# Summing the last three units of each expert stage with one-hot matmuls behind the loop, and one pair of modulation weights moved to the end of layer 0

## The chip, the cores and the metric

One core of one Trainium2 chip runs the whole kernel in one launch. The metric is the device time in microseconds. A core has TensorE (PE, with its weight loads shown apart as PEld), VectorE (DVE), ScalarE (ACT), GpSimd (POOL) and SyncE (SP, which here issues nearly all transfers). Each engine works through its own queue in order; semaphores tie the queues together.

## What is computed

Two layers over 256 latent and 256 context tokens of width 1024. Each layer has a mixer (an S5 state-space group, latent attention, an mLSTM group, then an output projection and a norm) and a mixture of 64 experts, top 8, with one shared expert. Both are modulated by rows that a small matmul makes from `c`. Cut to what matters here:

```python
for layer in range(DEPTH):
    mod_lat = silu(c) @ ada_w[layer] + ada_b[layer]
    mod_ctx = silu(c_ctx) @ ada_w[layer] + ada_b[layer]
    sh1, sc1, g1, sh2, sc2, g2 = split(mod_lat[:, None, :], 6)
    h_lat = _layer_norm(x_lat) * (1 + sc1) + sh1
    z_lat = h_lat @ w_in[layer]                    # projections, then S5, attention, mLSTM
    ...
    y_lat = concatenate([s5_lat, mla_lat, ml_lat]) @ w_out[layer]
    x_lat = _layer_norm(ALPHA * x_lat + g1 * y_lat, ln1_g[layer], ln1_b[layer])
    f_lat = _layer_norm(x_lat) * (1 + sc2) + sh2
    ffn_lat = _moe(f_lat, ...)                     # sum over a token's experts of gate * expert(f)
    x_lat = _layer_norm(ALPHA * x_lat + g2 * ffn_lat, ln2_g[layer], ln2_b[layer])
```

The context stream goes through the same steps in layer 0 and is not needed behind the mixer of layer 1. So the expert stage of layer 0 has 512 tokens (four tiles of 128), that of layer 1 has 256 (two tiles).

## The kernel before

**Units and scatters.** The router ranks the experts by load; `plan(l)` puts one to four ranks together into a *unit* of one or two tiles of at most 128 rows. Per unit POOL gathers the rows (L1779), PE makes gate and up (L1822) from expert weights that SP streams into the slots of `ring`, then down (L1835), and ACT and DVE write the gated rows to a tile `xo` (L1839, L1840). POOL then adds the rows of `xo` to the tokens' rows of `Y` in HBM by an indirect scatter with add (L1845), one for each expert's rows; each waits until the one before has landed. `units` is walked in the order of the plan. Over its last six turns `merging` puts alpha times the old rows and the shared expert's part times `g2` into `acc`.

**The last unit of layer 1.** Its rows are not scattered. `fold` makes one-hot tiles (128 rows by tokens), sums the rows per token on PE (L1914), multiplies by `g2` (L1915) and adds to `acc` (L1916). In layer 0 there is no such step.

**The loop.** `spilled` (L1924, L1925) is a loop over experts whose rows did not fit into the plan; it normally makes no turn. Its entry is passed by all engines together, when what stands ahead of it on each queue, the transfers included, is done. In layer 0 the program puts the last two scatters behind it.

**The combination.** `combine`, per tile of 128 tokens: SP loads its rows of `Y` (L2011), POOL multiplies them by `g2` (L2016), DVE adds `acc` and takes the row sums (L2019). The norm: mean on DVE (L416, L417), squares on ACT (L419), root on POOL (L420, L421), scale and shift on DVE (L427, L428). In layer 0 a second norm of the result follows, whose row ACT writes (L2030); PE transposes it (L313), and ACT and DVE modulate the transposed tile `hT` (L457, L459). The tiles run interleaved, each some steps behind the one before. Then PE does the projections of layer 1 (L466).

**Modulation.** `ada_pair(l, g)` makes two of the six modulation rows: eight steps, in each a load of 1 MB of `ada_w` by SP and four matmuls (L365). The loads share four places of 1 MB with the weights of the projections and of the output projection. In layer 1 `more` runs the pairs 1 and 2 inside the attention, and then loads `w_out`.

## Time and profile before

| | |
|---|---|
| median of 3 runs | 1956.22 us (1953.4 to 1962.03) |
| the profiled execution | 1952.31 us |
| span of its trace | 1950.3 us |
| PE busy | 1792.0 us, 92% |
| DVE, ACT, POOL busy | 775.7, 394.1, 453.5 us |
| mean granted clock of PE | 0.962 |

The profile comes from one execution. Its page gives each engine's busy time, the span in forty slices, the transfers, and the costliest groups of instructions by line. The trace behind it gives the timeline of a stretch: start, duration, engine, line, operation, tile written <- tiles read, and in brackets how long the engine had stood idle before and what ended that. xN says that N instructions of one kind stand in a row together. A granted clock of 1.00 is 2.4 GHz, one of 0.50 is 1.2 GHz. Names are those of the program; `cat`, `sw` and `spare` are buffers in which, at the end of a layer, rows of `Y` stand.

### The profile page before, as it was taken

Reading aid. Unit: us, or ns where it says so; the run is one execution under the profiler, and the core shown is the slowest. Engines: PE = TensorE matmul, PEld = TensorE weight load, DVE = VectorE, ACT = ScalarE, POOL = GpSimd, SP = SyncE. Lnnn points to the kernel's source line nnn. Section 1 sums busy time; section 2 is a strip of 40 time slices with the busy share of each in tenths; the row PEclk is TensorE's granted clock in tenths of the full one; section 3 lists DMA queues with packets and bytes.
Section 4 is the critical chain, followed back from the end, with each engine's and each line's share of the span. In section 5 each row is a group of like instructions: output and inputs, shape, how many; then the busy total and the mean of one; then the engine's idle time right before and its main releaser. Section 6 shows DMA issues by size and latency. Waiting matters only on the chain. (4 is left out here: it accounts for less than half of the span.)

```text
span 1950.3 us, 29070 instructions
## 1 busy us (share of the span) xinstructions
PE 1792.0 (92%) x10161; PEld 843.7 (43%) x10161; DVE 775.7 (40%) x2252; ACT 394.1 (20%) x756; POOL 453.5 (23%) x453
## 2 busy tenths in 40 slices
PE   6999999979999999999998089899899999999993
PEld 2654665533443433334332056665544444444330
DVE  5656664852422332222221386564722222322113
ACT  2345332301111111111111143531311111011000
POOL 3120211232232232223221570002011111112223
PEclk8999999989999999999999589899899999999997
DMA  8442568299999899999997425258599999996882
GB/s 327 143 98 102 180 242 304 81 337 348 342 335 336 323 304 350 371 352 350 341 365 269 130 74 107 97 217 307 189 417 366 350 345 332 340 370 200 320 296 88
DMA packets 158305, 523.98 MB, mean 269 GB/s; under 512 B 28862, under 2 KB 42110, under 8 KB 149452
## 3 DMA queue, kind: packets, MB, share of 16 engines
q1 hardware_dynamic: 139612, 480.36, 66.6%
q0 software_dynamic: 18544, 41.73, 9.7%
q8 instruction: 82, 1.34, 0.3%
q14 instruction: 67, 0.55, 0.1%
HBM read 531.12 MB, written 47.51 MB: 297 GB/s over the span
## 5 line engine op out<-in xcount | busy, mean ns | idle before, releaser
L1822 PE MATMUL gu<-ring,xT 128*32 128x512 f32 (+3 forms) x2896 | 653.4, 599 | 8.7 <-DMA ring<-in_exp_w 8.6
L1822 PEld LDWEIGHTS gu<-ring,xT 128*32 128x32 f32 (+3 forms) x2896 | 194.2, 128 | 372.0 <-issue 313.0
L1835 PE MATMUL dn<-ring,hT 128*32 128x512 f32 (+3 forms) x1448 | 319.2, 598 | 1.3 <-DVE hT L1726 1.0
L1845 POOL DMA_INDIRECT Y<-xo,gi x79 | 119.9, 1518 | 557.9 <-DMA Y<-xo,gi 129.0
L1718 DVE TENSOR_TENSOR hh<-gu,sg 128x256 f32<-128x256 f32 (+3 forms) x86 | 36.4, 425 | 496.5 <-ACT sg L1717 496.4
L1835 PEld LDWEIGHTS dn<-ring,hT 128*32 128x32 f32 (+3 forms) x1448 | 98.7, 128 | 178.3 <-issue 159.7
L1845 POOL DMA_INDIRECT Y<-xo,si x66 | 90.1, 1365 | 318.0 <-DMA Y<-xo,gi 216.5
L1840 DVE TENSOR_SCALAR xo<-dn,gc 128x512 f32<-128x512 f32 (+3 forms) x80 | 60.1, 751 | 229.5 <-PE dn L1835 221.4
L1717 ACT ACTIVATE sg<-gu 128x256 f32<-128x256 f32 (+3 forms) x86 | 32.8, 384 | 563.4 <-PE gu L1822 545.4
L466 PE MATMUL pT<-hT,w 128*128 128x512 f32 (+1 forms) x288 | 119.1, 566 | 2.5 <-ACT hT L457 2.5
L1797 PEld LDWEIGHTS <-fb 128*128 128x128 bf16 x1536 | 86.5, 99 | 55.0 <-issue 55.0
L1839 ACT ACTIVATE xo<-dn,gc 128x512 f32<-128x512 f32 (+3 forms) x80 | 55.0, 687 | 222.1 <-PE dn L1835 217.6
L1797 PE MATMUL xT<-oneh,fb 128*128 128x128 bf16 (+4 forms) x1536 | 97.3, 220 | 0.0
L1799 ACT COPY xT<-xT 128x512 f32<-128x512 f32 (+3 forms) x80 | 45.8, 573 | 219.4 <-PE xT L1797 137.4
L1429 PE MATMUL yo<-w,cat 128*128 128x512 f32 x192 | 83.3, 593 | 0.7 <-DMA w<-in_w_out 0.7
L1799 DVE COPY xT<-xT 128x512 f32<-128x512 f32 (+3 forms) x80 | 53.4, 670 | 76.5 <-PE xT L1797 43.6
L466 PEld LDWEIGHTS pT<-hT,w 128*128 128x128 f32 x288 | 55.4, 197 | 54.8 <-issue 48.0
L313 PE MATMUL hT<-cst,xt 128*128 128x128 f32 x64 | 14.0, 386 | 61.9 <-DMA w<-in_w_uv 50.8
L1779 POOL DMA_INDIRECT xg<-fd,gi x48 | 51.3, 1068 | 67.6 <-PE xT L313 33.7
L365 PE MATMUL ada<-w,sil 128*32 128x512 f32 x384 | 56.8, 650 | 10.4 <-DMA w<-in_ada_w 10.4
L474 PE MATMUL pN<-w,hT 128*128 128x256 f32 (+2 forms) x256 | 61.0, 395 | 0.0
L313 PEld LDWEIGHTS xT<-cst,xg 128*128 128x128 f32 (+4 forms) x384 | 41.1, 140 | 38.8 <-issue 36.3
(565 smaller groups left out, 2053.1 us busy)
## 6 DMA issues: line engine op xcount, KB each, us to landing
ring<-in_exp_w SPq DMA_DIRECT2D x768, 512.0 KB
w<-in_ada_w SPq DMA_DIRECT2D x48, 1024.0 KB
w<-in_w_out SPq DMA_DIRECT2D x8, 1024.0 KB
sw<-in_sh_w SPq DMA_DIRECT2D x2, 3072.0 KB
w<-in_w_uv SPq DMA_DIRECT2D x4, 1024.0 KB
Y<-zeros SPq DMA_DIRECT2D x8, 512.0 KB
w<-in_w_mm SPq DMA_DIRECT2D x4, 1024.0 KB
w<-in_w_qk SPq DMA_DIRECT2D x4, 768.0 KB
```

The source lines that it names most:

```text
L313: self.nc.tensor.transpose(out, in_, self.c("ident")[:in_.shape[0], :in_.shape[0]])
L365: nc.tensor.matmul(ps[32 * q:32 * q + 32, :], self.sil[:, k, :], t[:, q * 512:(q + 1) * 512], start=k == 0, stop=k == 7, tile_position=(0, ...
L466: self.nc.tensor.matmul(ps[base:base + m, n0:NT], w[k][:, col:col + m], hT[:, k, n0:NT], start=k == 0, stop=k == 7)
L474: self.nc.tensor.matmul(ps[:, :n], hT[:, k, i * 128:(i + 1) * 128], w[k][:, col:col + n], start=k == 0, stop=k == 7)
L1429: nc.tensor.matmul(st[at][n], cb[:, i * 128:(i + 1) * 128], wo[n][b], start=b == 0, stop=b == 7)
L1797: nc.tensor.matmul(o, self.fb[i][:, z, cs], t["oh"][:, i, 0:m], start=at == 0, stop=at + 1 == len(parts))
L1799: (nc.scalar.copy if hh else v.tensor_copy)(o, a)
L1822: nc.tensor.matmul(t["gu"][r, :], t["xt"][:, 2 * c + b, r], ws[j][:, b * 512:(b + 1) * 512], start=c == 0 and b == 0, stop=c == 3 and b == ...
L1835: nc.tensor.matmul(po[n][r, :], t["ht"][:, b, r], ws[b * nr + j][:, n * 512:(n + 1) * 512], start=b == 0, stop=b == 1, **kw)
L1839: nc.scalar.activation(xo[0:m, 0:512], po[0][0:m], AF.Identity, scale=t["gc"][0:m])
L1840: v.tensor_scalar(out=xo[0:m, 512:1024], in0=po[1][0:m], scalar1=t["gc"][0:m], scalar2=None, op0=OP.mult)
L1845: nc.gpsimd.indirect_dma_start(out=self.Y[l], out_offset=bass.IndirectOffsetOnAxis(ap=si[0:cap], axis=0), in_=xo[col:col + cap], in_offset ...
```

## The change

Constant `FOLD = 3`: the rows of the last three units of either layer are not scattered. In layer 0 that takes away four scatters, in layer 1 five (its last unit was not scattered before either).

When the third unit from the end has had its turn, what is left of `merging` is drained, POOL itself issues the loads of `Y` (four in layer 0, two in layer 1), and `add_y` on POOL multiplies each by `g2` and adds it to `acc`. `backs` makes the one-hot tiles on DVE in the last turn. Behind the loop `fold` sums the three units' rows per token on PE, six matmuls per tile, DVE writes them times `g2` into the tile's place, and the sum with `acc` follows as before.

The ring's pool is closed right behind the loop. At the end of layer 0 the pools of layer 1 open there, and the pair (1, 1) of modulation is run interleaved with the combination; the small constants and the first projection weights are loaded behind its weights. In the attention of layer 1 only the pair (1, 2) is left. Some pools of layer 1 open later or close later.

```diff
+FOLD = 3
...
+            self.zp, self.gp = P(zs, "z"), P(zs, "gates")
...
-        for j, g in ((0, 1), (0, 2), (1, 0)) if l == 0 else ((1, 1), (1, 2)):
+        for j, g in ((0, 1), (0, 2), (1, 0)) if l == 0 else ((1, 2),):
...
-                if l and u is units[-1]:
+                if u in units[-FOLD:]:
                     t["xo"] = xo
                     continue
...
-        for _ in merge:
-            pass
+            if i == n - FOLD:
+                for _ in merge:
+                    pass
+                for k, y in enumerate(self.yb):
+                    nc.gpsimd.dma_start(y, self.Y[l][k * 128:(k + 1) * 128])
+                for add in self.adds:
+                    add()
+            if i == n - 1:
+                self.backs(l, units[-FOLD:], rp, len(self.yb))
...
+    def backs(self, l, units, rp, nt):
+        v = self.nc.vector
+        for k, t in enumerate(t for u in units for t in u["tiles"]):
...
+            for i0 in range(0, nt, 2):
+                v.tensor_scalar(out=t["back"][0:m, i0:i0 + 2], in0=self.c("iota1")[0:m, 0:256].rearrange("p (a b) -> p a b", a=2),
+                                scalar1=128.0 * i0 - 4097.0, scalar2=at[0:m], op0=OP.add, op1=OP.is_equal)
...
+    def add_y(self, y, acc, g2):
+        p = self.nc.gpsimd
+        p.tensor_tensor(out=y, in0=y, in1=g2, op=OP.mult)
+        p.tensor_tensor(out=acc, in0=acc, in1=y, op=OP.add)
+
+    def fold(self, i, units, g2):
...
+        ts = [t for u in units for t in u["tiles"]]
+        y = self.yb[i]
+        for n in range(2):
+            ps, cs = self.bank("fold"), slice(n * 512, (n + 1) * 512)
+            for x, t in enumerate(ts):
+                nc.tensor.matmul(ps, t["back"][0:t["m"], i], t["xo"][0:t["m"], cs], start=x == 0, stop=x + 1 == len(ts))
+            v.tensor_tensor(out=y[:, cs], in0=ps, in1=g2[:, cs], op=OP.mult)
...
-            if last:
-                self.fold(l, units[-1], rp, acc, sw, tiles)
             self.spilled(l, fT, acc, sw, rp, ring, tiles)
...
+            er.close()
+            ahead = iter(())
+            if not last:
+                self.begin(l + 1)
+                self.ada = self.ada_pair(l + 1, 1, self.adp)
+
+                def ahead():
+                    for k in range(8):
+                        next(self.ada)
+                        if k % 2:
+                            yield
+                    self.fetch(l + 1)
+                ahead = ahead()
+            with self.tc.tile_pool(name=f"comb{l}", bufs=1) as pp:
+                weave(*(self.combine(l, i, t, pp, self.yb[i], acc, sw, 2 * i, len(tiles), units[-FOLD:]) for i, t in enumerate(tiles)), ahead)
+                if not last:
+                    weave(self.ada)
...
-        nc.sync.dma_start(a, self.Y[l][i * 128:(i + 1) * 128])
-        for _ in range(lag):
+        for _ in range(i):
             yield
-        if l == 0 and i == 1:
-            self.fetch(l + 1)
-        nc.gpsimd.tensor_tensor(out=a, in0=a, in1=sw[:, 2 if t >= 2 else 3], op=OP.mult)
-        yield
+        self.fold(i, units, sw[:, 2 if t >= 2 else 3])
+        for _ in range(lag - i):
+            yield
```

In the order of the instructions, POOL at the end of layer 0 looked like this before: scatters from `xo` (`gi` and `si` are the lists of rows), the loop (L1924, L1925) and two more scatters; behind these, after three memsets, come the products of the combination (L2016).

```order
L1845 DMA Y_78<-xo,si 640x1024
L1845 DMA Y_78<-xo,gi 640x1024 x2
L1924 TENSOR_LOAD ovl
L1925 COMPARE_AND_BRANCH
L1925 UNCONDITIONAL_BRANCH x2
L2078 BRANCH_PREFETCH_HINT
L1925 REGISTER_ALU
L1925 COMPARE_AND_BRANCH
L1925 UNCONDITIONAL_BRANCH
L1845 DMA Y_78<-xo,gi 640x1024
L1845 DMA Y_78<-xo,si 640x1024
```

Now the last scatters are followed by four loads of `Y` (L1892) and the eight products and sums of `add_y` (L1925, L1926), and the loop (L1945) stands behind them.

```order
L1850 DMA Y_78<-xo,gi 640x1024
L1850 DMA Y_78<-xo,si 640x1024
L1892 DMA cat_1334<-Y_78 128x1024 x3
L1892 DMA sw<-Y_78 128x1024
L1925 TENSOR_TENSOR cat_1334<-cat_1334,sw 128x1024 x2
L1926 TENSOR_TENSOR acc<-acc,cat_1334 128x1024 x2
L1925 TENSOR_TENSOR cat_1334<-cat_1334,sw 128x1024
L1925 TENSOR_TENSOR sw<-sw 128x1024
L1926 TENSOR_TENSOR acc<-acc,cat_1334 128x1024
L1926 TENSOR_TENSOR acc<-acc,sw 128x1024
L1945 TENSOR_LOAD ovl
```

So POOL's products moved from behind the loop to ahead of it, its sums are new, and four scatters are gone.

PE leaving that loop, before: the transposes of the combination's rows (L313), then the projections of layer 1.

```order
L1925 REGISTER_ALU
L1925 COMPARE_AND_BRANCH
L1925 UNCONDITIONAL_BRANCH
L313 MATMUL hT<-cst,xt 128x128 x32
L466 MATMUL pT<-hT,w 128x512 x16
L474 MATMUL pN<-w,hT 128x256 x16
```

And now, where L1936 are the summing matmuls (six for a tile), L367 the modulation matmuls (four for a step), and L315 the transposes:

```order
L1936 MATMUL fold<-xo,xT 128x512 x6
L367 MATMUL ada<-w,sil 32x512 x4
L1936 MATMUL fold<-xo,xT 128x512 x3
L367 MATMUL ada<-w,sil 32x512 x4
L1936 MATMUL fold<-xo,xT 128x512 x3
L367 MATMUL ada<-w,sil 32x512 x8
L315 MATMUL hT<-cst,xt 128x128 x8
L1936 MATMUL fold<-xo,xT 128x512 x6
L367 MATMUL ada<-w,sil 32x512 x8
L1936 MATMUL fold<-xo,xT 128x512 x6
L367 MATMUL ada<-w,sil 32x512 x4
L315 MATMUL hT<-cst,xt 128x128 x4
```

Four more modulation matmuls, the other twenty transposes and the projections follow. All summing and all eight steps now stand ahead of most transposes; eight transposes of the first tile stand ahead of the third and the fourth tile's summing.

SP behind the same loop now begins with modulation weights and the stores of `x2d` (L2049); the weights of the projections (L354) come behind them.

```order
L365 DMA w<-in_ada_w 128x2048 x4
L2049 DMA x2d<-acc 128x1024
L365 DMA w<-in_ada_w 128x2048 x2
L2049 DMA x2d<-acc 128x1024
L365 DMA w<-in_ada_w 128x2048 x2
L1239 DMA cols<-in_cols 128x20
L1240 DMA mlg<-in_ml_g 128x256
L354 DMA w<-in_w_uv 128x2048 x2
L354 DMA w<-in_w_go 128x1344 x2
L2049 DMA x2d<-acc 128x1024 x2
```

Before, four loads of `Y`, the small constants and two of these weights stood there first.

## Rows read from the trace of the kernel before

**Rows 1.** The page: part 1 (busy us, share, instructions), a line of part 2 (forty slices).

```profile
PE 1792.0 (92%) x10161; PEld 843.7 (43%) x10161; DVE 775.7 (40%) x2252; ACT 394.1 (20%) x756; POOL 453.5 (23%) x453
...
GB/s 327 143 98 102 180 242 304 81 337 348 342 335 336 323 304 350 371 352 350 341 365 269 130 74 107 97 217 307 189 417 366 350 345 332 340 370 200 320 296 88
```

**Rows 2.** Stretch: length; busy us of PE, PEld, DVE, ACT, POOL; clock, DMA, GB/s.

```profile
1080.00:1120.00 40.00, 1.05 (x5) 1.05 (x6) 17.70 (x27) 7.31 (x11) 21.70 (x18) 0.50 0.49 147
```

**Rows 3.** Timeline, end of layer 0: start, us, engine, line, tiles, [idle before <-releaser].

```profile
1065.81 2.34 PE L1835 MATMUL dn<-ring,hT 128*32 128x512 f32 x20
...
1073.22 1.44 POOL L1845 DMA_INDIRECT Y<-xo,gi  x1 [2.94 <-DMA Y<-xo,si]
...
1092.51 1.37 POOL L1845 DMA_INDIRECT Y<-xo,si  x1 [4.41 <-DMA Y<-xo,gi]
...
1095.87 1.28 SPq L2011 DMA_DIRECT2D cat<-Y  x3
```

**Rows 4.** Waits of SP from 1040 to 1100: us in total, times, longest.

```profile
SPq L1925 <- DMA Y<-xo,gi: 12.3, 2, 7.1
...
SPq L2011 <- DMA Y<-xo,si: 10.4, 1, 10.4
```

**Rows 5.** Timeline of the combination behind layer 0.

```profile
1099.16 7.92 POOL L2016 TENSOR_TENSOR cat<-cat,sw 128x1024 f32<-128x1024 f32 x3 [2.63 <-DMA cat<-Y]
...
1101.54 3.34 DVE L2019 SCALAR_TENSOR_TENSOR cat<-cat,acc 128x1024 f32<-128x1024 f32 x1 [32.48 <-DMA cat<-Y]
...
1109.81 2.33 POOL L2016 TENSOR_TENSOR sw<-sw 128x1024 f32<-128x1024 f32 x1
...
1116.11 0.57 POOL L421 TENSOR_TENSOR a0rs<-a0rs,mhalf 128x1 f32<-128x1 f32 x1
...
1117.48 1.22 DVE L2019 SCALAR_TENSOR_TENSOR sw<-sw,acc 128x1024 f32<-128x1024 f32 x1
...
1117.65 1.24 ACT L2030 ACTIVATE xt<-acc,nb,a0rs 128x1024 f32<-128x1024 f32 x1 [0.62 <-DVE nb L2029]
...
1118.95 1.97 PE L313 MATMUL hT<-cst,xt 128*128 128x128 f32 x8 [50.80 <-DMA w<-in_w_uv]
...
1133.56 15.79 PE L466 MATMUL pT<-hT,w 128*128 128x512 f32 x32
```

**Rows 6.** The page, part 5 (busy us, mean ns of one): POOL's gathers.

```profile
L1779 POOL DMA_INDIRECT xg<-fd,gi x48 | 51.3, 1068 | 67.6 <-PE xT L313 33.7
```

**Rows 7.** Timeline at the end of layer 1.

```profile
1904.51 1.34 POOL L1845 DMA_INDIRECT Y<-xo,gi  x1 [6.20 <-DMA Y<-xo,si]
...
1914.19 3.70 PE L1914 MATMUL fold<-xo,xT 128*128 128x512 f32 x8 [0.84 <-ACTq L1925]
...
1915.18 1.51 POOL L1845 DMA_INDIRECT Y<-xo,gi  x1 [1.91 <-DMA Y<-xo,si]
...
1915.35 0.69 DVE L1915 TENSOR_TENSOR sw<-fold,sw 128x512 f32<-128x512 f32 x1 [1.10 <-PE fold L1914]
...
1924.32 0.81 SPq L2011 DMA_DIRECT2D cat<-Y  x2
...
1932.67 1.23 DVE L2019 SCALAR_TENSOR_TENSOR cat<-cat,pz 128x1024 f32<-128x1024 f32 x1 [12.04 <-POOL cat L2016]
...
1941.12 1.28 DVE L428 SCALAR_TENSOR_TENSOR pz<-cat,c1rs,sw 128x1024 f32<-128x1024 f32 x1 [0.46 <-POOL c1rs L421]
```

**Rows 8.** Timeline at the end of layer 1's attention.

```profile
1332.51 0.73 POOL L1194 TENSOR_TENSOR hs<-hs,mlg 128x256 f32<-128x256 f32 x1 [0.54 <-DVE hs L1088]
...
1334.10 2.77 PE L365 MATMUL ada<-w,sil 128*32 128x512 f32 x22
...
1337.61 27.73 PE L1429 MATMUL yo<-w,cat 128*128 128x512 f32 x64 [0.74 <-DMA w<-in_w_out]
```

**Rows 9.** The start of layer 1's projections, columns as in rows 2.

```profile
1137.00:1138.00 1.00, 1.00 (x3) 0.52 (x2) 1.00 (x1) 0.99 (x3) 0.92 (x2) 0.85 0.00 0
```

**Rows 10.** Inside layer 1's attention, columns as in rows 2.

```profile
1300.00:1320.00 20.00, 20.00 (x157) 15.26 (x156) 14.35 (x46) 6.88 (x17) 4.59 (x7) 1.00 0.39 130
```

60 lines of the change are left out of this document (21 added, 39 removed).

## The prediction

> **What bounds the kernel now.** I read the busy shares first, then busy time and clock by stretches, then the two places where those show PE empty, then the order of events there. PE is busy for 92% of the span [rows 1], so a microsecond counts where PE stands still or where PE's own queue is shortened. The change works at three places: the end of layer 0, the end of layer 1, and the attention of layer 1, from which it takes modulation work.
>
> At the end of layer 0, PE works 1.05 us in the 40 us from 1080 to 1120, at a clock of 0.50, the lower of its two levels (1.2 of 2.4 GHz) [rows 2]. The events say why. PE's last down matmul ends at 1065.81 + 2.34 = 1068.15; the scatters of the last units follow on POOL, each waiting until the one before has landed, up to 1092.51 [rows 3]. SP waits for them, first at the loop for spilled experts (12.3 us in two of its waits), then, behind it, 10.4 us ahead of its loads of Y [rows 4]. The last scatter lands at 1095.87, where SP issues these loads [rows 3]. From there products, sums and norms lead to the first transposes at 1118.95 and the projections of layer 1 at 1133.56 [rows 5]. Thus the chain is scatters, loop, scatters, loads of Y, combination. Weights are not missing there.
>
> **End of layer 0, up to the loop.** Removed: four scatters, those issued from 1073.22 on. Put there: four loads of Y that POOL issues itself, and eight 128x1024 products and sums on POOL, all ahead of the loop. The loop holds each engine until POOL is through, so POOL's new work must be priced whole. An issue: 1.07 us, from POOL's gathers [rows 6]. The first load starts at 1073.22, when the last kept scatter has landed; from SP's issue to the first product took 1099.16 − 1095.87 = 3.29 us [rows 3, 5], so it is there by 1076.5, before the fourth issue ends at 1073.22 + 4 × 1.07 = 1077.5. A product alone: 2.33 us (the group of three takes 7.92 beside DVE's adds; that is 2.64 each) [rows 5]. Eight: 18.6 us. POOL ends at 1096.1; with 0.3 us to leave the loop, PE may begin at B = 1096.4 (by 2.64 each, 1098.9). Before, the loads of Y were issued at 1095.87. So **removing four scatters brings this point forward by nothing**: the products which stood behind the loop now stand ahead of it. SP too leaves the loop only then, so the ring's place, though given back right behind the loop, takes its first modulation weights no sooner than SP issued its loads of Y before.
>
> POOL's issues run beside DVE's last work. A scatter issued while DVE evacuated a sum took 1.51 us, one without took 1.34 [rows 7]; I add nothing for that 0.17, four times 0.7 us at most.
>
> The Trainium skill (SBUF — State Buffer, section "SBUF: two separate sides") warns that a transfer issued from POOL can be held for as long as DVE runs in a mode that takes both shared ports. Were each of the four issues held by one DVE instruction of 0.69 us [rows 7], B would be 2.8 us later; the 0.17 us of the row speaks against it.
>
> **Behind the loop.** Added on PE: six summing matmuls per token tile, 24 in all. The same shape elsewhere: 64 records in 27.73 us, two records to a matmul (four summing matmuls make eight), so 0.87 us each [rows 7, 8]; at the lower clock twice that, 1.73. PE has then been still for 28 us, so it starts at 0.50; in the trace of before the clock rose within 1137 to 1138 (0.85 on the mean there), some 4 us after the projections began [rows 5, 9]. The first six: 4 us at the low level (2.3 matmuls), 3.7 matmuls at the high one, 3.2 us: B + 7.2. Bounds 5.2 and 10.4. The evacuation is 0.69 [rows 7]: B + 7.9.
> Then tile 0's chain up to its transposes: sum 1.3, mean 0.3, squares 1.3 (ACT writes a row of this size in 1.24), root 0.9 (its second step on POOL 0.57), scale and shift 1.28, the same mean, squares and root again 2.5, the normalised row 1.24 [rows 5, 7]: about 9.2 us with reads and hand-overs. Before, it took 1118.95 − 1101.54 = 17.4, since POOL's products ran beside the sums (3.34 against 1.22 alone) [rows 5]; those are gone, and I take 9.6 with DVE's other evacuations in between. First transposes at B + 17.5 (before: 23.1 us after 1095.87).
> But PE's queue puts tile 0's eight transposes (2 us) ahead of the third tile's sum, and this and eight modulation matmuls ahead of the fourth's: B + 19.5, + 5.2 = 24.7, + 2.1 = 26.8, + 5.2 = 32.0. Evacuated at 32.7, chain 9.2, transposes 1.8: projections at B + 43.7 = 1140.1, against 1133.56: **+6.5 us**. The modulation matmuls otherwise fill PE's gaps (four in 1.0 us, see below). Their 8 MB come at some 340 GB/s as in the expert stages [rows 1], 24.7 us, and the first step that needs more than the first four MB comes at B + 24.7. On SP the last four of these loads stand behind the stores of tiles 0 and 1, which wait for their norms (B + 14 and B + 19), and the weights of the projections (4 MB) stand behind all of them and need places that the last four steps free, the last at about B + 33: they are in by B + 37, ahead of B + 43.7. Bounds: +2 (all summing at the high level, no queueing of tile 3 behind tile 0) and +10 (the products at 2.64, the first six at the low level).
>
> **Attention of layer 1.** Moved out: eight steps of modulation, each eight records; 22 such records took 2.77 us, so 1.0 us a step and 8.1 in all [rows 8]. PE is full there, 20.00 of 20 us [rows 10]. At its end PE waits for POOL's last step of the head sums (ends 1333.24), then 2.77 us of modulation and 0.74 us of waiting for the output weights stand ahead of the output projection [rows 8]. Both go for sure, 3.5 us: the remaining pair moves up eight places, and the output weights with it. Of the other five steps only a part counts, since that POOL step waits on DVE (0.54) [rows 8], whose chain does not get shorter. I take **−4.5** (−2, if PE's gaps there lower the clock, to −8.9 with all 8.1 and the wait).
>
> **End of layer 1.** Removed: five scatters, those from 1904.51 on. Ahead of the loop now: two POOL loads, four products and sums. 1904.51 + 3.29 = 1907.8, + 4 × 2.33 + 0.3 = 1917.4. There the loop is left; before, SP issued the loads of Y at 1924.32 and the first sum behind the loop stood at 1932.67 [rows 7]. Behind the loop: twelve summing matmuls, 10.4 us; before, four took 3.70 [rows 7] ahead of the loop, hidden under scatters, and this cover is gone for all twelve. Then evacuation 0.7, and from the second tile's add to the end of its last step 7.1 us (before, from 1932.67 to 1942.40, 9.7 for both tiles at once; the first is now six matmuls ahead) [rows 7]: 1917.4 + 18.2 = 1935.6, −6.8. PE stands still for 4 us ahead of that; at layer 0's end the clock had fallen by 1080 [rows 2], and 4 us of low clock cost 2 us: −4.8. I take **−5.7** (−7.5 to −3.5).
>
> Small one-hot tiles on DVE: six and three instructions of 256 columns beside the last units' matmuls, when DVE is mostly idle; nothing.
>
> **Sum.** Against the profiled execution's 1952.31: +6.5 − 4.5 − 5.7 = −3.7, 1948.6. The median is 3.9 above that execution; the same −3.7 gives 1952.5. Runs of before spread over 8.6 us, so that 0.5% (9.8 us) is about what a measurement of this kernel can tell from no change.
>
> **Rivals.** *The summing stays at the low level* (slower). Between B and the projections PE would work in pieces of 5 to 7 us between waits; with pieces of 2 us from 1118.95 on the clock rose only at 1137 [rows 5, 9]. Then tile 0's six cost 3.2 more, the third and fourth tiles' 10.4 more, the steps between 2: +15.6 behind layer 0, and up to 10.4 at the end of layer 1. With half of the latter: 1952.5 + 20 = 1972; it decides if the clock is not back by the sixth matmul. For it: the 0.50 up to 1120 [rows 2]; against: it rose behind back-to-back matmuls of this width at 1133.56. Chance 0.15.
> *The boundary costs nothing*: the loop is passed while POOL still adds, or tile 3 is not queued behind tile 0. −10.2: 1946.0. For it: the program's own weaving; against: SP's wait at the loop behind POOL's work [rows 4]. Chance 0.17.
> *All the modulation comes back*: PE bound through the attention, −8.9 there: 1948.1. For it 20.00 of 20; against, POOL's step waits for DVE. Chance 0.13.
> That the ring's place gives no earlier weights is in the forecast.
>
> **How the numbers follow.** Forecast 0.55. Faster by over 0.5%: half of the second rival, a third of the third, a tenth of the forecast with its bounds added: 0.09 + 0.04 + 0.06, with a little for both rivals together: 0.22. Slower: 0.12 of the first, 0.02 of the forecast's upper bounds. The range takes the lower bounds of two terms (−11.5) and the upper of all (+10): 1941 to 1963; 0.15 of the first rival lies above, 0.03 below.
>
> **What would show it.** POOL's last sum ahead of the loop ends near 1096; first summing matmul follows within 0.5 us; clock 1.00 within its first six; first transposes near 1114, projections near 1140; the output projection of layer 1 starts 199.5 us after the projections, against 204.0 (1337.61 − 1133.56); last step of the second tile about 18 us after the second loop. The forecast is wrong if the loop is left before POOL's sums, if the clock stays low, or if the attention shrinks by 8 us.

## The result

The changed kernel has a median of 1973.52 us (1969.75 to 1977.43), the kernel before 1955.99 beside it: a ratio of 1.0084 with an interval of 1.0067 to 1.0101, **slower by about 17 us**. The forecast was 1952.5 with a range up to 1963. The profiled execution of after took 1974.91 us (span 1973.1), 22.6 more than that of before. Where these 22.8 us of span lie, measured between the same events in both traces:

| stretch | before | after | difference | forecast |
|---|---|---|---|---|
| up to the end of the last down matmul of layer 0 | 1068.15 | 1069.67 | +1.5 | 0 |
| from there to the projections of layer 1 | 65.4 | 81.9 | +16.5 | +6.5 |
| projections to PE's first matmul of `ss` (the S5 stage, below) | 75.4 | 83.4 | +8.0 | 0 |
| from there to the start of the output projection | 128.7 | 123.8 | −4.9 | −4.5 |
| output projection, its first 64 records | 27.6 | 29.1 | +1.5 | 0 |
| experts of layer 1, up to the last `xo` | 549.1 | 550.0 | +0.9 | 0 |
| from the last `xo` to the end | 36.1 | 35.2 | −0.8 | −5.7 |

The S5 stage is the work of the state-space group behind its projections; `ss` is the sum of squares for a norm, which the latent attention makes next. These two rows bound the stage, in before and in after:

```profile
1208.91 1.12 PE L826 MATMUL ss<-za,ones 128*128 128x512 f32 x2 [1.15 <-ACT za L825]
...
1234.91 1.12 PE L828 MATMUL ss<-za,ones 128*128 128x512 f32 x2 [1.15 <-ACT za L827]
```

PE's busy time grew by 39 us. Most of it is the new summing matmuls, and a part of that their low clock: 72 records take 44.5 us on the page of after, and would take 31 at the 0.43 us of [rows 8].

```profile
PE 1830.8 (93%) x10225; PEld 859.7 (44%) x10225; DVE 780.1 (40%) x2271; ACT 394.6 (20%) x756; POOL 455.7 (23%) x456
...
L1936 PE MATMUL fold<-xo,xT 128*128 128x512 f32 (+3 forms) x72 | 44.5, 762 | 34.7 <-POOL acc L1926 27.7
```

**End of layer 0.** POOL's timeline of after answers to [rows 3] and [rows 5] (columns as there):

```profile
1074.49 1.75 POOL L1892 DMA_DIRECT2D cat<-Y  x3 [2.23 <-DMA Y<-xo,si]
...
1078.58 4.63 POOL L1925 TENSOR_TENSOR cat<-cat,sw 128x1024 f32<-128x1024 f32 x2 [1.81 <-DMA cat<-Y]
...
1094.66 2.33 POOL L1926 TENSOR_TENSOR acc<-acc,sw 128x1024 f32<-128x1024 f32 x1
```

The eight products and sums take 18.4 us, and PE's first summing matmul starts 0.4 us behind them, at 1097.38 (B of the prediction, 1096.4). PE behind it, two records to a matmul:

```profile
1097.38 8.56 PE L1936 MATMUL fold<-xo,xT 40*128 40x512 f32 x12 [27.71 <-POOL acc L1926]
...
1117.86 1.09 PE L315 MATMUL hT<-cst,xt 128*128 128x128 f32 x8 [2.14 <-ACT xt L2055]
1118.88 10.72 PE L1936 MATMUL fold<-xo,xT 40*128 40x512 f32 x12
...
1131.57 6.01 PE L1936 MATMUL fold<-xo,xT 40*128 40x512 f32 x12
...
1149.79 1.97 PE L315 MATMUL hT<-cst,xt 128*128 128x128 f32 x8 [5.10 <-ACT xt L2055]
1151.55 8.63 PE L468 MATMUL pT<-hT,w 128*128 128x512 f32 x17
```

The third tile's six take 10.72 us where the fourth's take 6.01. The stretches show the clock (columns as in [rows 2]):

```profile
1097.00:1101.00 4.00, 3.62 (x4) 1.33 (x5) 0.00 (x0) 0.00 (x0) 0.52 (x1) 0.50 0.68 227
1101.00:1103.00 2.00, 2.00 (x4) 0.44 (x2) 0.00 (x0) 0.00 (x0) 0.00 (x0) 0.59 0.98 414
1103.00:1107.00 4.00, 4.00 (x15) 1.17 (x16) 1.68 (x3) 0.00 (x0) 0.00 (x0) 1.00 1.02 430
...
1119.00:1128.00 9.00, 9.00 (x11) 3.00 (x12) 4.65 (x10) 2.68 (x6) 2.67 (x4) 0.54 0.74 269
```

It rose by 1103, fell again behind the 2.14 us in which PE waited for the first tile's row, and was at 0.54 over the nine microseconds of full work from 1119.

**The S5 stage.** Behind the transposes POOL and DVE make tables (`cmA`, `cmB`, `KT`, `MT`) that PE multiplies with the projected rows. POOL in after:

```profile
1151.89 0.13 POOL L1292 MEMSET va<- 128x16 f32 x1 [3.68 <-PE hT L315]
1152.09 1.05 POOL L694 TENSOR_TENSOR cmA<-pz 128x512 f32<-128x512 f32 x1
```

A small memset of `va`, whose place in memory opens later now, stands ahead of the tables and waits until PE has made its last transposes. In before the tables began 1.7 us ahead of the projections, now 0.5 behind them. PE later waits 6.14 us ahead of the second group's products `kk`, for a copy of `va` that stands in DVE's queue among DVE's tables:

```profile
1189.12 1.11 PE L651 MATMUL kk<-KT,pz 64*32 64x128 f32 x32 [6.14 <-DVE va L1307]
```

2.2 us of lateness became 8 us, and on the way there DVE's tables came to end later, 38.9 us behind the start of the projections instead of 32.1. POOL's table `MT` of the third group waits for the products `m`, which PE makes some 22 us behind the projections. In before POOL comes to this point early and pauses, and eight of DVE's 24 table products take 0.69 us in that time; in after POOL comes late, only four take so little, and the other twenty take 1.2 to 1.8 us beside POOL's products. In before, DVE and POOL:

```profile
1152.95 0.69 DVE L629 TENSOR_TENSOR cmA<-pz,pmc 128x512 f32<-128x512 f32 x1
...
1157.28 1.80 POOL L692 TENSOR_TENSOR MT<-cmA,cmB 128x512 f32<-128x512 f32 x1 [5.64 <-PE m L313]
```

and in after:

```profile
1174.55 1.52 POOL L694 TENSOR_TENSOR MT<-cmA,cmB 128x512 f32<-128x512 f32 x1 [2.08 <-PE m L315]
...
1176.66 1.43 DVE L631 TENSOR_TENSOR cmA<-pz,pmc 128x512 f32<-128x512 f32 x1
```

No run takes POOL's and DVE's tables apart, so this part is read from traces.

**End of layer 1**, POOL and PE of after, to be held against [rows 7]:

```profile
1927.91 1.21 POOL L1892 DMA_DIRECT2D cat<-Y  x2 [6.09 <-DMA Y<-xo,si]
1933.92 2.39 POOL L1925 TENSOR_TENSOR cat<-cat,sw 128x1024 f32<-128x1024 f32 x1 [4.80 <-DMA cat<-Y]
...
1941.12 2.34 POOL L1926 TENSOR_TENSOR pz<-pz,cat 128x1024 f32<-128x1024 f32 x1
```

```profile
1943.96 13.14 PE L1936 MATMUL fold<-xo,xT 96*128 96x512 f32 x24 [7.00 <-POOL pz L1926]
```

The loads take 6.0 us from issue to the first product, the twelve matmuls 13.14 us. The second tile's last evacuation on DVE then stands behind the first tile's last step:

```profile
1957.51 1.28 DVE L430 SCALAR_TENSOR_TENSOR pz<-cat,c0rs,sw 128x1024 f32<-128x1024 f32 x1 [0.79 <-POOL c0rs L423]
1958.71 0.68 DVE L1937 TENSOR_TENSOR cat<-fold,sw 128x512 f32<-128x512 f32 x1
...
1964.21 1.28 DVE L430 SCALAR_TENSOR_TENSOR pz<-cat,c1rs,sw 128x1024 f32<-128x1024 f32 x1 [0.77 <-POOL c1rs L423]
```

### The profile page after: what moved, and what is told of

It is laid out like the page before. It is cut to its first block, busy times and chain, and to the rows that moved or that the text cites. A ratio compares the mean times of both kernels' runs of the same rounds, so it can differ in the third digit from the quotient of the medians.

```text
span 1973.1 us, 29187 instructions
## 1 busy us (share of the span) xinstructions
PE 1830.8 (93%) x10225; PEld 859.7 (44%) x10225; DVE 780.1 (40%) x2271; ACT 394.6 (20%) x756; POOL 455.7 (23%) x456
## 4 chain that ended last, share of the span: by engine, by line
PE 66%; DMA 10%; DVE 9%; issue 6%; POOL 5%; ACT 3%; SPq 0%; POOLq 0%; ACTq 0%; DVEq 0%
PE gu L1827 24%; PE dn L1840 12%; DMA ring<-in_exp_w 4%; PE pT L468 4%; DMA Y<-xo,si 3%; PE xT L1802 3%; PE pN L476 2%; PE yo L1434 2%; PE xT L315 2%; PE ada L367 2%; PE fold L1936 2%; PE s L918 2%; PE o L939 2%; PE hT L315 1%; POOL Y L1850 1%
## 5 line engine op out<-in xcount | busy, mean ns | idle before, releaser
L1827 PE MATMUL gu<-ring,xT 128*32 128x512 f32 (+3 forms) x2896 | 653.9, 601 | 12.9 <-DMA ring<-in_exp_w 12.7
L1850 POOL DMA_INDIRECT Y<-xo,gi x74 | 111.6, 1507 | 539.6 <-DMA Y<-xo,gi 107.7
L1850 POOL DMA_INDIRECT Y<-xo,si x62 | 84.7, 1366 | 309.2 <-DMA Y<-xo,gi 211.9
L1804 DVE COPY xT<-xT 128x512 f32<-128x512 f32 (+3 forms) x80 | 53.4, 670 | 77.8 <-PE xT L1802 44.5
L1936 PE MATMUL fold<-xo,xT 128*128 128x512 f32 (+3 forms) x72 | 44.5, 762 | 34.7 <-POOL acc L1926 27.7
L1784 POOL DMA_INDIRECT xg<-fd,gi x48 | 52.2, 1088 | 64.8 <-PE xT L315 32.4
L367 PE MATMUL ada<-w,sil 128*32 128x512 f32 x384 | 55.6, 648 | 10.9 <-DMA w<-in_ada_w 10.9
L476 PE MATMUL pN<-w,hT 128*128 128x256 f32 (+2 forms) x256 | 62.7, 404 | 0.0
L315 PEld LDWEIGHTS xT<-cst,xg 128*128 128x128 f32 (+4 forms) x384 | 41.1, 140 | 38.8 <-issue 36.3
```

The costliest lines, as they stand in the source:

```text
L315: self.nc.tensor.transpose(out, in_, self.c("ident")[:in_.shape[0], :in_.shape[0]])
L367: nc.tensor.matmul(ps[32 * q:32 * q + 32, :], self.sil[:, k, :], t[:, q * 512:(q + 1) * 512], start=k == 0, stop=k == 7, tile_position=(0, ...
L476: self.nc.tensor.matmul(ps[:, :n], hT[:, k, i * 128:(i + 1) * 128], w[k][:, col:col + n], start=k == 0, stop=k == 7)
L1804: (nc.scalar.copy if hh else v.tensor_copy)(o, a)
L1827: nc.tensor.matmul(t["gu"][r, :], t["xt"][:, 2 * c + b, r], ws[j][:, b * 512:(b + 1) * 512], start=c == 0 and b == 0, stop=c == 3 and b == ...
L1850: nc.gpsimd.indirect_dma_start(out=self.Y[l], out_offset=bass.IndirectOffsetOnAxis(ap=si[0:cap], axis=0), in_=xo[col:col + cap], in_offset ...
```

## The experiments

All runs in one table: median; ratio to the kernel before on the same chip, with its interval; and from the profiled execution, in us: from layer 0's last down matmul to the projections, and to POOL's first S5 table; the S5 stage; from layer 1's last `xo` to the end of the last step.

| run | median | ratio | proj. | tables | S5 | layer-1 end |
|---|---|---|---|---|---|---|
| before | 1956.22 | | 65.4 | 63.7 | 75.4 | 28.1 |
| after | 1973.52 | 1.0084 [1.0067, 1.0101] | 81.9 | 82.4 | 83.4 | 27.6 |
| e1_va | 1965.27 | 1.0045 [1.0022, 1.0068] | 80.3 | 78.6 | 75.0 | 26.7 |
| e2_ada | 1973.51 | 1.0078 [1.0048, 1.0108] | 90.3 | 88.0 | 74.4 | 28.0 |
| e3_adds | 1957.14 | 1.0001 [0.998, 1.0022] | 70.5 | 71.0 | 82.9 | 20.5 |
| e4_folds | 1973.85 | 1.0081 [1.005, 1.0111] | 78.0 | 83.2 | 89.4 | 29.0 |
| c1_warm | 1970.85 | 1.0082 [1.005, 1.0114] | 81.5 | 81.7 | 79.9 | 27.2 |
| c2_va_adds | 1956.72 | 0.9994 [0.9974, 1.0014] | 75.9 | 74.1 | 79.0 | 20.5 |
| c3_va_ysum | 1957.49 | 1.001 [0.9991, 1.0029] | 71.2 | 69.4 | 75.1 | 22.7 |
| c4_folds | 1958.38 | 1.0011 [0.999, 1.0032] | 70.9 | 76.8 | 83.9 | 22.6 |
| d1_l1only | 1953.77 | 0.9985 [0.9974, 0.9996] | 70.2 | 68.5 | 76.8 | 22.0 |
| d2_l1_ada | 1961.1 | 1.0021 [1.001, 1.0033] | 71.4 | 79.0 | 91.6 | 24.5 |
| d3_third | 1960.02 | 1.0018 [1.0005, 1.0032] | 68.4 | 71.9 | 82.5 | 27.1 |
| d4_l1_before | 1949.91 | 0.9968 [0.9954, 0.9981] | 64.4 | 62.7 | 75.9 | 22.0 |
| d5_l1_ada_pmc | 1961.9 | 1.0026 [1.0014, 1.0038] | 70.2 | 77.1 | 84.3 | 22.0 |
| d6_folds_pmc | 1974.09 | 1.0087 [1.0052, 1.0122] | 77.5 | 83.2 | 83.8 | 26.8 |
| d7_c4_pmc | 1959.76 | 1.0013 [0.9995, 1.0031] | 67.2 | 73.4 | 84.3 | 24.3 |
| f1_ada_x2d | 1956.38 | 0.9996 [0.9979, 1.0013] | 70.0 | 70.4 | 80.9 | 22.5 |
| f2_c4_x2d | 1954.5 | 0.9987 [0.997, 1.0003] | 63.1 | 64.5 | 80.5 | 24.4 |

The median is over many executions, the other columns come from one of them, and executions of one kernel differ by up to 20 us. The profiled one lies off its median by 9.3 us in d2 (above), 4.7 in e4 and 4.2 in c2 (above), and by about 3 in e1 and d6 (below). A difference of 2 or 3 us between two rows of these columns says little. They leave out what comes ahead of layer 0's last down matmul, and the attention.

### One part at a time

**e1_va**: the memset of `va` on DVE.

```diff
-        nc.gpsimd.memset(va[:, :, :, 64], 1.0)
+        (nc.vector if l else nc.gpsimd).memset(va[:, :, :, 64], 1.0)
```

> The changed kernel with one edit: layer 1's small memset of va (16 columns) is issued by DVE instead of POOL. Theory A: in the changed kernel this memset stands on POOL ahead of the S5 tables and waits for the last transposes (POOL idle 3.68 us, until 1151.89), so POOL's table products begin 2 us later against the projections and run in step with DVE's products on the same port; PE then waits 6.14 us for DVE's copy of va. Then the time from the first projection to the first wait of the S5 sums (75.3 us in the kernel before, 83.4 in the changed one) falls to about 75, and the time falls by 8 us to 1965.5. Theory B: the step comes from the rest of the moved modulation (its row memset on POOL and its sum on DVE stand between the tables); then it stays at 83 us and the time at 1973.

1965.27, 8.2 below after. POOL's tables no longer wait for PE:

```profile
1146.63 1.05 POOL L694 TENSOR_TENSOR cmA<-pz 128x512 f32<-128x512 f32 x1 [1.60 <-ACT xt L2055]
```

The S5 stage is back at 75.0. The place of one memset in a queue cost 8 us.

**e2_ada**: the pair (1, 1) back in the attention.

```diff
-        for j, g in ((0, 1), (0, 2), (1, 0)) if l == 0 else ((1, 2),):
+        for j, g in ((0, 1), (0, 2), (1, 0)) if l == 0 else ((1, 1), (1, 2)):
...
-                self.ada = self.ada_pair(l + 1, 1, self.adp)
```

> The changed kernel with the modulation pair (1, 1) put back into layer 1's attention; the summing matmuls stay. Theory A (the summing and its clock cost the boundary, the modulation little): the stretch from leaving the loop of layer 0 to the projections stays within 3 us of its 54.2, and the attention's end goes back by 3 to 5 us (2.77 us of modulation and 0.74 us of waiting ahead of the output projection come back); time 1973.5 + 2, 1975. Theory B (the modulation matmuls and their loads hold the boundary): the stretch falls by 10 us or more, the time to 1966 or less.

1973.51, as after; the parts moved apart. Without modulation between the sums, PE waits 5.25 us ahead of the first transposes and the last twelve summing matmuls run low all through:

```profile
1122.10 20.36 PE L1936 MATMUL fold<-xo,xT 40*128 40x512 f32 x24
```

```profile
1120.00:1140.00 20.00, 19.80 (x28) 7.07 (x28) 6.86 (x18) 5.36 (x10) 2.55 (x6) 0.51 0.06 26
```

That lost 8.4 us at the boundary, while the S5 stage gained 9 (the memset comes off the path in this order). From the first sum to the projections 62.3 us passed, where theory A had 54 and theory B less than after; the attention grew by 5.2 us, as A had it. So the pair at the boundary was no net load there; that it bridged pauses of PE is the reading of this trace.

**e3_adds**: POOL's sums behind the loop instead of ahead of it.

```diff
                     nc.gpsimd.dma_start(y, self.Y[l][k * 128:(k + 1) * 128])
-                for add in self.adds:
-                    add()
...
+            for add in self.adds:
+                add()
```

> The changed kernel with POOL's sums of Y into acc written behind the loop; its products by g2 stay ahead of it. Theory A (the loop holds every engine until POOL is through): the first summing matmul of layer 0 comes 9.3 us earlier (four sums of 2.33 us), that of layer 1 up to 4.7 us earlier, and PE's idle times in front of them shrink from 27.7 and 7.0 us by as much; time 1973.5 - 12, 1961.5. Theory B (the loop's own transfers or the barrier's semaphores set the moment, or the sums only move the wait to DVE's add behind the loop): the first projection moves by under 3 us, time 1971 to 1974.

1957.14: −16.4, more than the 12 that were expected, and in the places that the theory names: −11.4 at the boundary and −7.1 at the end of layer 1. PE's pause ahead of the sums shrinks from 27.71 to 17.39 us, and at the end of layer 1 from 7.00 to 2.17, behind which the twelve take 10.58 instead of 13.14:

```profile
1086.21 11.50 PE L1934 MATMUL fold<-xo,xT 40*128 40x512 f32 x12 [17.39 <-POOL sw L1923]
...
1926.76 10.58 PE L1934 MATMUL fold<-xo,xT 96*128 96x512 f32 x24 [2.17 <-POOL cat L1923]
```

**e4_folds**: all 24 summing matmuls first, in one block.

```diff
+                for i, t in enumerate(tiles):
+                    self.fold(i, units[-FOLD:], sw[:, 2 if t >= 2 else 3])
...
-        for _ in range(i):
-            yield
-        self.fold(i, units, sw[:, 2 if t >= 2 else 3])
-        for _ in range(lag - i):
+        for _ in range(lag):
             yield
```

> The changed kernel with all summing matmuls put first behind the loop (24 in a row in layer 0), ahead of the modulation and the transposes. Theory A (in the changed kernel PE's queue makes the third and the fourth tile's sums wait for the first tile's transposes, and the pause ahead of these drops the clock for the third tile's six, 10.7 us): 24 matmuls take about 23.5 us (5 us at 0.50, the rest at 1.00), the first projection comes about 38 us behind the loop instead of 54.2; time 1973.5 - 16, 1957.5. Theory B (the norms of four tiles on DVE, ACT and POOL set the pace): the first projection comes at 49 us or later; time 1968 or more.

1973.85. That is theory B's outcome. The block takes 29.45 us, and the clock rises only some 12 us into it:

```profile
1095.17 29.45 PE L1936 MATMUL fold<-xo,xT 40*128 40x512 f32 x48 [26.96 <-POOL acc L1926]
```

The projections come 4 us earlier all the same, and the S5 stage grows to 89.4, which no theory had. POOL's tables there wait 4.76 us for a store of `x2d`. d5 to f2, below, take that up.

### Is it the clock?

**c1_warm**: matmuls without use keep PE busy up to the sums, 30 in layer 0 and 7 in layer 1, and 4 ahead of the last tile's transposes.

```diff
+            for _ in range(7 if last else 30):
+                nc.tensor.matmul(ps, t["back"][0:t["m"], 0], t["xo"][0:t["m"], 0:512], start=True, stop=True)
```

> The changed kernel with PE kept at work where it waits: matmuls of the summing's shape whose result nobody reads, 30 ahead of the loop of layer 0 (26 us at the high level, from the last rows to the loop's exit), 4 ahead of the last transposes there, 7 ahead of the loop of layer 1. Theory A (the lower clock level is what made the summing dear): the first six take 5.2 to 5.5 us instead of 8.6, the twelve of layer 1 10.4 to 10.7 instead of 13.1, the third tile's six 5.2 instead of 10.7 if the clock then also holds through the wait for the first transposes; time 1973.5 - 6 to - 11, 1963 to 1968. Theory B (the norms' chain sets the pace at either place): the clock reads 1.00, but the projections and the last step come within 3 us of where they were; time 1971 or more.

1970.85, near theory B's time. In layer 1 the clock held: twelve in 10.58 instead of 13.14 us, and 19.0 us from leaving the loop to the end of the last step instead of 21.5. (The loop was left 2.1 us later there, so the end came only 0.4 sooner.) In layer 0 it did not, although it was at 1.00 up to the first sum:

```profile
1071.24 26.02 PE L2019 MATMUL warm<-xo,xT 128*128 128x512 f32 x60 [0.84 <-ACT xo L1844]
1099.40 11.44 PE L1936 MATMUL fold<-xo,xT 40*128 40x512 f32 x12 [2.14 <-issue]
```

```profile
1085.00:1099.00 14.00, 12.26 (x29) 5.13 (x27) 0.00 (x0) 0.00 (x0) 12.81 (x7) 1.00 0.03 6
...
1101.00:1107.00 6.00, 6.00 (x7) 1.67 (x6) 0.69 (x1) 0.00 (x0) 0.00 (x0) 0.50 1.01 426
1107.00:1113.00 6.00, 6.00 (x14) 1.74 (x14) 2.06 (x5) 0.00 (x0) 0.00 (x0) 0.50 0.38 157
```

A pause of 2.14 us was followed by 13 us at the low level under full work, a pause of 1.97 us in layer 1 by none. So the matmuls do run at the low level, but keeping PE busy beforehand doesn't reliably prevent it.

**d3_third**: in layer 0 only the last of three one-hot tiles is summed (two matmuls per tile instead of six; the rows of the other two are left out).

```diff
+        if len(self.yb) == 4:
+            ts = ts[-1:]
```

> The changed kernel with a third of the summing in layer 0: only the last unit's rows are summed there (two matmuls per tile instead of six, 8 instead of 24), those of the other two units are left out of the result. Theory A (PE's summing, its place in the queue and its clock make the stretch from the loop to the projections): that stretch falls from 54.2 us to about 37. Theory B (the norms' steps on DVE, ACT and POOL set it): 48 us or more.

From the first sum to the projections 41.4 us instead of 54.2; median −13.5:

```profile
1098.48 3.78 PE L1938 MATMUL fold<-xo,xT 128*128 128x512 f32 x4 [27.04 <-POOL acc L1926]
```

That lies between theory A's 37 and B's 48. So the sixteen matmuls taken out carry 12.8 us of the boundary: PE's work lies on its path, though not alone.

### Both at once

**c2_va_adds**: e1_va and e3_adds together.

> The changed kernel with both edits, DVE's memset of va and POOL's sums of Y behind the loop. If the two prices are separate (8.2 and 16.4 us), 1973.5 - 24.6, 1949; then it is 8 us faster than the kernel before. If the S5 tables fall into step again or the sums behind the loop hold what the memset frees, 1955 to 1957.

1956.72, no better than e3 alone: its S5 stage takes 79.0 against 82.9, but its projections come 5.4 us later. The gains do not add; c2's profiled execution lay 4.2 us above its median, so how far the columns explain it stays open.

**c3_va_ysum**: c2, and POOL makes no products or sums: DVE adds the rows of `Y` to the sums as it reads them from PSUM.

```diff
-            v.tensor_tensor(out=y[:, cs], in0=ps, in1=g2[:, cs], op=OP.mult)
+            v.tensor_tensor(out=y[:, cs], in0=ps, in1=y[:, cs], op=OP.add)
+        v.tensor_tensor(out=y, in0=y, in1=g2, op=OP.mult)
```

> The changed kernel with DVE's memset of va and without POOL's products and sums at all: DVE adds the folded rows to Y as it reads them from PSUM, multiplies the row by g2 (1.22 us) and goes on as before. Theory A (what the loop waits for sets the boundary): the loop of layer 0 is left when the loads of Y have landed, 1.5 to 2 us behind the last issue, some 18 us earlier than in the changed kernel and 8 us earlier than with the products ahead of it; DVE has 1.22 us more per tile; time 1949 - 6, 1943. Theory B (behind an earlier loop PE's low clock and the norms' chain take the gain back): within 2 us of the run with both edits, 1947 to 1951.

1957.49: PE starts its sums 14.15 us behind the down matmul, half of after's 27.71, but then needs 57.0 us to the projections (after 54.2). The time is neither theory's. **c4_folds** is c3 with the block of e4:

> As the run without POOL's products and sums, with all summing matmuls first behind the loop. Alone, this order gained nothing (1973.85 against 1973.52): PE was through 12 us earlier, but the last tile's norm took 18 us from its sum to its transposes, queued behind other tiles' steps on ACT and DVE. Theory A (that queue sets the pace): within 3 us of the run without it. Theory B (the earlier sums pay once the loop is left earlier): 5 us or more faster.

1958.38, within 3 us of c3 as theory A had it. The clock:

```profile
1083.00:1100.00 17.00, 16.71 (x18) 5.01 (x18) 3.84 (x5) 0.00 (x0) 0.50 (x1) 0.50 0.65 255
```

An earlier start here met 17 us of low clock; then the tables are late again. That c3 and c4 come out alike for A's reason isn't shown.

### The end of layer 1 alone

**d1_l1only**: the pools and the early close of the ring stay, layer 0 scatters all its rows as before, the pair is back in the attention, sums behind the loop, `va` on DVE.

```diff
-                if u in units[-FOLD:]:
+                if l and u in units[-FOLD:]:
```

> One part alone: layer 0 scatters all its units as the kernel before does, with the modulation pair back in the attention; layer 1 sums its last three units behind the loop, with POOL's sums of Y behind the loop too and DVE's memset of va. Theory A (the change loses in layer 0 and wins in layer 1 once POOL's sums are behind the loop): from the last rows to the last step 20.5 us, as in the run with the sums behind the loop, against 28.15 in the kernel before, all else as before; 1956.5 - 7.7 = 1949. Theory B (what layer 1 gained there came from the earlier parts of that run): 1955 or more.

1953.77, between the two theories. The boundary is still 4.8 us longer than before, though its scatters are the same. SP issues two weight loads just ahead of one of them, and in this trace that one lands late:

```profile
1088.04 0.90 SPq L354 DMA_DIRECT2D w<-in_w_uv  x2
```

```profile
1088.25 1.49 POOL L1850 DMA_INDIRECT Y<-xo,gi  x1 [6.50 <-issue]
...
1099.17 1.38 POOL L1850 DMA_INDIRECT Y<-xo,si  x1 [8.89 <-DMA Y<-xo,gi]
```

The same wait was 4.41 us in before [rows 3], and 3.96 in d4 (below), where no such loads stand there. **d2_l1_ada** adds the pair of modulation at the boundary:

> As the run with layer 1 alone, but with the modulation pair (1, 1) run beside layer 0's combination as the change has it, without any summing there. Theory A (the pair itself costs nothing at the boundary, where PE stands still anyway, and shortens the attention): from the last down matmul of layer 0 to the projections within 2 us of the 65.4 of the kernel before, the attention with its wait 4 to 5 us shorter (the output projection's first matmuls at the lower level give back 1.5); 1949 - 3.5 = 1945. Theory B (its loads and places hold the projections' weights, or the transposes wait behind it on PE): the boundary 4 us or more longer, 1949 or more.

1961.1, near theory B, and the boundary is 6.0 us longer than before, as B had it. The attention gives 5.4 us, but 5.2 come back between the output projection and the experts. The S5 stage takes 91.6, in an execution 9.3 us above the median.

**d4_l1_before**: the kernel before with only the new end of layer 1, sums behind the loop.

```diff
+            if l and i == n - FOLD:
...
+                    nc.gpsimd.dma_start(y, self.Y[l][k * 128:(k + 1) * 128])
...
+                for y, a, g in self.adds:
+                    nc.gpsimd.tensor_tensor(out=a, in0=a, in1=y, op=OP.add)
```

> The kernel before with one part of the change alone: layer 1's last three units are summed behind the loop, with POOL's products ahead of it and its sums behind it. Layer 0, its boundary and the mixer are the kernel before's. Theory A (layer 1's end gives 7.7 us, 20.5 instead of 28.15 from the last rows to the last step, and the 4.8 us that the earlier run with layer 1 alone lost at layer 0's boundary came from weight loads that ran beside a scatter): 1957 - 7.7 = 1949. Theory B (the end gives less, as that run's 22.0 already shows): 1951 to 1954.

**1949.91, 0.9968 [0.9954, 0.9981]: 0.3% faster than before, and faster than after.** From the last `xo` to the end of the last step 22.0 us pass, 6.1 less than in before; the time is theory A's, the 22.0 theory B's:

```profile
1904.85 1.22 POOL L1889 DMA_DIRECT2D cat<-Y  x2 [6.53 <-DMA Y<-xo,si]
1911.69 4.69 POOL L1891 TENSOR_TENSOR cat<-cat,sw 128x1024 f32<-128x1024 f32 x2 [5.62 <-DMA cat<-Y]
1917.00 4.64 POOL L2013 TENSOR_TENSOR pz<-pz,cat 128x1024 f32<-128x1024 f32 x2 [0.62 <-POOL cat L1891]
```

Only the products stand ahead of the loop; the sums (L2013) run beside PE's matmuls.

### What eats an early projection

**d5_l1_ada_pmc** (d2), **d6_folds_pmc** (e4 with e1) and **d7_c4_pmc** (c4) put the load of the S5 constants `pmc` ahead of four small loads of biases in program order.

> As the run with layer 1 summed and the modulation pair at layer 0's boundary, with one edit: the S5 constants of layer 1 are loaded ahead of the projections in program order. Theory A (in that run SP's load of them stood behind the projections' first store, DVE's tables began 11.85 us behind the projections' start instead of 2.1, and PE waited for DVE): the stage shrinks from 91.6 us to 75 to 77, time 1961.1 - 15, 1946. Theory B (POOL's late start is the cause): it stays above 85, time 1958 or more.

> As the run with all summing first (1973.85), with DVE's memset of va and the S5 constants loaded ahead of the projections in program order. Theory A (that run hid its earlier boundary behind S5 tables that began 15.5 us behind the projections' start): the stage shrinks from 89.4 to 76, time 1973.9 - 13, 1961, 4 below the run with the memset alone. Theory B: 1965 or more, the order of the summing is worth nothing.

> As the run without POOL's products and sums and with all summing first (1958.38), with the S5 constants loaded ahead of the projections in program order. Theory A: the stage shrinks from 83.9 to 76, time 1958.4 - 8, 1950. Theory B: 1956 or more.

1961.9, 1974.09 and 1959.76: none gained. In d6 and d7 SP issues the biases behind `pmc`; in d5's trace they still come ahead of it, from 1139.81 on, so d5 does not do what it was meant to. What holds the tables stands in that trace too, on SP and on POOL:

```profile
1136.05 2.71 SPq L354 DMA_DIRECT2D w<-in_w_go  x2
1138.82 0.90 SPq L2063 DMA_DIRECT2D x2d<-acc  x2
...
1147.05 0.36 SPq L623 DMA_DIRECT2D pmc<-in_s5m  x1
```

```profile
1147.12 1.05 POOL L698 TENSOR_TENSOR cmA<-pz 128x512 f32<-128x512 f32 x1 [10.74 <-DMA x2d<-acc]
```

The last two stores of `x2d` stand in SP's queue behind projection weights which wait for the modulation's places. The tables and `pmc` wait for these stores to land. **f1_ada_x2d** (d5) and **f2_c4_x2d** (d7) let POOL issue these stores:

```diff
-        nc.sync.dma_start(d["out"][(t - 2) * 128:(t - 1) * 128] if last else self.x2[t * 128:(t + 1) * 128], x2)
+        q = nc.gpsimd if i > 1 and not last else nc.sync
+        q.dma_start(d["out"][(t - 2) * 128:(t - 1) * 128] if last else self.x2[t * 128:(t + 1) * 128], x2)
```

> The kernel of d5_l1_ada_pmc (the kernel before with the new end of layer 1, the pair of modulation at the end of layer 0, and the S5 constants loaded ahead of the biases), but the stores of the last two tiles' rows to x2d are issued by POOL right after their norms, instead of by SP behind the projections' weights. In d5 the projections started 70.2 us after the last down matmul, but POOL's S5 tables, whose place in SBUF held those rows, waited 10.74 us for these stores and started only at 77.1; from the projections to the first S5 wait it took 84.3 us against 75.4 in the kernel before. Theory A (the stores' place in SP's queue holds the tables, and the tables' start sets the end of the S5 stage): tables start at about the projections' start (68 to 70 us behind the last down matmul), the stage takes 75 to 77 us, median 8 us below d5: about 1953 to 1954. Theory B (the tables are held by SP's own load of their constants, which stays behind the weights and the biases): that load starts some 3 us earlier at most, the stage takes 81 us or more, median about 1959.

> The kernel of d7_c4_pmc (the new kernel with POOL's sums replaced by DVE's sums out of PSUM, va's constant on DVE, all summing first, S5 constants ahead of the biases), with the stores of the last two tiles' rows to x2d issued by POOL. In d7 POOL's tables waited 9.64 us for these stores and started 73.4 us behind the last down matmul, the projections at 67.2; stage 84.3 us; median 1959.76. Theory A as for f1_ada_x2d: tables start at 66 to 68, the stage takes 76 to 78 us, median about 1952 to 1953. Theory B: stage 81 us or more, median 1957 or more.

1956.38 and 1954.5, 5.5 and 5.3 below d5 and d7. In f1:

```profile
1131.03 0.65 POOL L2064 DMA_DIRECT2D x2d<-acc  x1
...
1139.66 1.05 POOL L698 TENSOR_TENSOR cmA<-pz 128x512 f32<-128x512 f32 x1 [4.27 <-ACT hT L459]
```

The tables start with the projections, as theory A said, but the stage only falls to 80.9; f1's and f2's times lie between A and B too. DVE's first table in f1 stands in its queue behind a copy of projected rows, which waits for ACT.

```profile
1147.34 0.42 DVE L731 COPY us<-pT 128x256 f32<-128x256 f32 x1 [3.83 <-ACT us L730]
...
1148.28 0.98 DVE L635 TENSOR_TENSOR cmA<-pz,pmc 128x512 f32<-128x512 f32 x1
```

In all the runs of the table the stage ends 77 to 84 us after POOL's first table (tables subtracted from projections plus stage), whatever the projections do. Where the tables begin ahead of the projections, by 1.7 to 2.3 us, the stage takes 74.4 to 79.0; where they begin behind them or together, 79.9 to 91.6.

## Why the prediction was wrong, point by point

The step that failed is "Behind the loop", with the path cut off at its end. It gave the third tile's six matmuls the high clock level and forecast +6.5 at the boundary; they ran at the low level again, and +16.5 came. The stage behind the projections was put at nothing, and +8.0 came there. At the end of layer 1 the mechanism was right and the size was not: −0.5 for −5.7 up to the end of the last step (the table's row goes on to the end of the program). These three make 23.2 of the 26 us by which the profiled execution misses 1948.6.

- **The loop is held by POOL's sums: right.** First sum at 1097.38 against B = 1096.4; the 1.3 us were there already at the last scatter's landing. The rival that the boundary costs nothing falls, and e3_adds confirms the mechanism by its −16.4. The four issues took 2.3 us, where 4 × 1.07 were taken. That they would run beside DVE's work was wrong: DVE had been idle since 1070.57, 32.4 us ahead of its first evacuation at 1103.01, so that the question of the shared port did not arise. The 0.17 us of [rows 7] is no mark of DVE's work either: the scatter at 1073.22 in [rows 3] took 1.44 us with DVE idle since 1069.05.
- **Behind the loop: the step that failed at the boundary.** Forecast B + 43.7, measured B + 54.2. The first six took 8.6 us (7.2, within its bounds). The first tile's transposes came at B + 20.5 (17.5). The third six, priced at 5.2 as "at the high level", took 10.7, the fourth 6.0. From the last tile's add to its transposes 11.5 us passed, 9.2 were taken. The starts, 2.0; the third six, 5.5; the fourth, 0.8; the chain, 2.2: that is the 10.5. The upper bound of +10 left out that the clock can fall a second time. Besides, the range does not follow from the bounds given: all three lower bounds together lie 10.7 us below the forecast, all three upper ones 8.2 above it, where −11.5 and +10 were used.
- **The rival "stays at the low level"** gave 1972, near the measured 1973.5, but not by its own point of decision: the clock was back within the first six and fell again behind a wait of 2.14 us that the forecast itself had put there. What low clock cost over the forecast: about 7.7 us behind layer 0 (1.4, 5.5, 0.8), 2.6 at the end of layer 1 (13.14 against 10.58), up to 1.5 in the output projection; some 12 of the 26 us, without what it cost in the S5 stage. The Trainium skill (TensorE: Matmul & The Clock Gate, section "A second HAM failure mode: psum-queue depth-cycling") describes a bf16 kernel in which short idle times between groups of matmuls make the clock swing between its levels, with a loss in throughput; the 0.54 from 1119 to 1128 behind a pause of 2.14 us is such a swing, c1_warm's 10.58 us behind a pause of 1.97 us shows none.
- **The S5 stage was not priced: +8.0.** The prediction followed each queue up to the projections and stopped there. POOL's queue was followed only ahead of the loop; the memset of `va` behind it was neither in the sum nor a rival. e1_va shows that the memset's place is the whole of the 8 us; how 2.2 us of lateness become 8 is read from the traces (POOL's pause and DVE's tables, above).
- **Attention: right, but part of it is given back.** Of −4.5, the 3.5 at its end came as 3.0 (the wait ahead of the output projection shrank from 4.3 to 1.3), and 1.9 from the other steps. The rival of −8.9 falls. From the start of the output projection to the first matmul of an expert unit, however, 67.7 us passed in after and 65.5 in before: +1.5 in the first 64 records, and a wait of PE for DVE's row `f` that before does not have (shown below). In e2, d1 and d4, where the pair stays in the attention, this stretch takes 65.2 to 65.5 us; in the runs that move it, 67.7 to 70.7, with such a wait in each. So the pair's move is worth less than its −4.9; the forecast had nothing for what comes back.

```profile
1402.90 1.90 PE L315 MATMUL fT<-cst,f 128*128 128x128 f32 x8 [3.63 <-DVE f L1452]
```

- **End of layer 1: mis-sized, −0.5 for −5.7.** Loads to first product took 6.0 us for the 3.29 of [rows 5], the loop was left 16.0 us after their issue (12.9 taken), and from there to the end of the last step 21.5 us passed (18.2). Of these 3.3 us the low clock is some 2.5, since c1_warm, at the high level, has 19.0; what is left is DVE's queue, in which the second tile's evacuation waits for the first tile's last step. d4_l1_before shows that 6 us lie there, if the sums go behind the loop.

**What stays open:** why the clock rises after 4 us in one run and after 17 in another, and so why c2, c3 and c4 gain nothing from an earlier start; the traces tell the level, not the cause. Pauses of about 2 us stand ahead of both outcomes. That the S5 stage follows its tables is shown for `va` (e1) and the stores (f1, f2); that DVE's queue is the rest of f1's 80.9, and that DVE's tables take longer beside POOL's, is read from traces alone.

## What to carry to other kernels

Follow a moved piece of work past the point where the path seems to rejoin: each queue's next stage may hang on a memset, a store or a place in memory that the move pushes back, and its first instruction (here POOL's first table) tells more than the milestone in between. Work put ahead of a barrier that all engines pass counts whole, even on an idle engine; d4 keeps ahead of it only what fills waits. And price matmuls that come behind a pause at both clock levels, each group anew.
